# Overlapped dilated and neighbourhood attention: values copied in DRAM by blocks of 32 columns, dilated values in two loads, a later bias fill and two staging tiles

## Chip, cores and metric

The kernel runs on one core of one Trainium2 chip. The metric is the device time of one execution in microseconds (us), compared as the median of several runs. An execution is also profiled, and every row below is from that one.

## The reference

A whole two-block network on 1024 tokens of width 1024. The first block (retention, a state space branch, cross attention) is not touched. The second block projects the normalised tokens to queries, keys and values of two attentions with 8 heads each, normalises both outputs, multiplies them by `w_out`, and ends with a mixture of experts:

```python
p_dil = proj[..., :3 * WIDTH_DIL].reshape(B, S, 3, N_HEADS_DIL, HEAD_DIM).transpose(2, 0, 3, 1, 4)
p_na = proj[..., 3 * WIDTH_DIL:].reshape(B, S, 3, N_HEADS_NA, HEAD_DIM).transpose(2, 0, 3, 1, 4)
y_dil = dilated_mixture_attention(p_dil[0], p_dil[1], p_dil[2], slopes)
y_na = neighbourhood_attention(p_na[0], p_na[1], p_na[2], rpb[layer])
y_dil = rms_norm_2(y_dil.transpose(0, 2, 1, 3).reshape(B, S, WIDTH_DIL), g_out_dil[layer])
y_na = rms_norm_2(y_na.transpose(0, 2, 1, 3).reshape(B, S, WIDTH_NA), g_out_na[layer])
h = h + jnp.concatenate([y_dil, y_na], axis=-1) @ w_out[layer]
```

The dilated attention lets a token see keys at distances 1, 4 and 16 apart inside windows. The neighbourhood attention lays the tokens on a grid of 16 rows by 64 columns; a token sees 8 rows by 16 columns, with a learned bias for each offset.

## The kernel before

Everything in float32, by three matmuls per product (a high part and a low part of each operand: `mm3`, lines 181 to 183). Heads are worked in four pairs. A scheduler orders each engine's instructions by a simulated timeline, so that work of one function stands between that of others; each engine then takes its own list strictly in order.

Around the change, in order of time:

- `na_bias` (line 1281) builds the table of biases on GpSimd and writes it to DRAM: `e_scr` (the learned values) and `b_scr` (all biases and -1e30 where nothing is seen). `na_bias_row` copies 16 rows from `e_scr` to `b_scr`. All these transfers are issued by GpSimd, while `values` makes the dilated values tile by tile (`v_f`) and SyncE stores them to `vd_scr`.
- `dilated` (line 1091) loops over pairs. In a round it scores the present pair (`scores`, 16 pieces: 8 windows of 32 positions, then 8 of the 4 residues), and turns, splits and multiplies the pair before (`scale` on GpSimd, `flip`, `gather`). `load_values` (line 1145) fetches the values of a piece from `vd_scr` into a tile `dv`; 3 are fetched a round ahead, the others 3 steps ahead. `project` makes the next pair's queries and keys, and `filler` other work: in round 0 the neighbourhood's values, stored to `vn_scr`; in rounds 1 to 3 its queries and keys (`na_project`), each through the tile `n_`, of which there is one.
- After pair 3 is scored, the last dilated round runs beside `neighbour` (line 1317): 32 steps (2 blocks of rows, 4 pairs, 4 blocks of columns), each scores, softmax, turn (`flip` into `npT`, 3 tiles) and multiply (`gather`). For a step `load_values` (line 1346) fetches a tile `nv` from `vn_scr`, 8 ahead. Each pair's output goes through a tile `nyo` that takes a buffer of `npT`, and is stored to `yn_scr` by SyncE. `mix_out2` multiplies by `w_out` in between.

SyncE issues nearly all loads and stores, in one list. A load into a buffer in use holds up what is behind it. The two loads that the change is about read

```python
src = vt[:, lo:hi, z.pr].rearrange("(c r) x f -> r x c f", r=2)                                    # dv, L1152
src = v_scr[pr].rearrange("(r x) c i f -> r x c (i f)", x=64)[:, k0s[j % 4]:k0s[j % 4] + 32, rb:rb + 3]  # nv, L1350
```

so that the outermost dimension of the source has 2 steps for a `dv` of a window and 4 for an `nv`.

Of the kernel before, what the change touches and what calls it, by code (L numbers as in the profile page):

```python
# [10 lines left out]
F32 = mybir.dt.float32  # L11
# [108 lines left out]
class Net:  # L120
# [970 lines left out]
    def dilated(self, hn, v_scr, yd_scr, g, acc, filler):  # L1091

        nc = self.nc
        with ExitStack() as es:
# [144 lines left out]
            def tiles():  # L1239
                sq, o = (wk.tile([P, 2, 512], F32R, name=name, tag="dpT", bufs=3) for name in ("dsq", "dyo"))  # L1240
                return sq[:, 0].bitcast(F32), o

            def spare():
                sq = wk.tile([P, 2, 2, 256], F32, name="dsq", tag="db2", bufs=1).rearrange("p a b x -> p (a b x)")[:, :512]
                return sq, single("dyo")

            def single(name):
                return cp.tile([P, 2, 512], F32R, name=name, tag="n_")

            prev = None  # L1250
            for pr in range(PAIRS + 1):
# [30 lines left out]
                filler(pr, lambda: wk.tile([P, 2, 2, P], F32R, name="v_f", tag="dv", bufs=6), single)  # L1282
                prev = z


    def na_bias(self, e_scr, b_scr):


        nc = self.nc
        with self.pool("nb", 1, side="right") as wk:  # L1290
# [15 lines left out]
            nc.gpsimd.memset(neg, NEG)  # L1306
            for half, r0, r1, k0 in ((0, 0, 8, 8), (0, 5, 8, 0), (1, 0, 8, 0), (1, 0, 4, 8)):
                to = b_scr[:, half, 16 * r0:16 * r1, k0:k0 + 4].rearrange("q p r t k -> p q (r t k)")
                nc.gpsimd.dma_start(to, neg[16 * r0:16 * r1, None].to_broadcast(list(to.shape)))

    def na_bias_row(self, e_scr, b_scr, row):

        half, r = divmod(row, 8)
        rs = min(max(row - 4, 0), 8)
        self.nc.gpsimd.dma_start(b_scr[:, half, 16 * r:16 * r + 16, rs - 4 * half:rs - 4 * half + 8].rearrange("q c r t k -> q c (r t k)"),
                                 e_scr[:, :, rs - row + 7:rs - row + 15].rearrange("q c r h t k -> q c (r h t k)"))

    def neighbour(self, qn_scr, kn_scr, v_scr, yn_scr, b_scr, g, acc):

        nc = self.nc  # L1320
        with ExitStack() as es:
            cp = es.enter_context(self.pool("nc", 1, side="left"))
            qp = es.enter_context(self.pool("nq", 2, side="left"))
            k0s = (0, 8, 24, 32)
            sets = [(cp.tile([P, 2, 12, 64], F32R, name=f"nkbd{i}"), cp.tile([P, 12, 2, 3, 32], F32, name=f"nbias{i}")) for i in range(2)]
# [102 lines left out]
    def mix_out2(self, wk, res, x3_scr, y_scr, acc, ready):  # L1428
# [13 lines left out]
        for side in range(2):  # L1442
# [3 lines left out]
            for n in range(NT):  # L1446
                y = coming
                if n + 1 < NT:
                    coming = fetch(side * NT + n + 1)
                if n % 4 == 0:  # L1450
                    r = self.rsqrt_mean(acc[side][:, n:n + 4], 512)
                for cb in range(2):
                    cs = slice(cb * 512, cb * 512 + 512)
                    po = self.bank("m")
                    self.mm3(po, lambda k: (y[k][:, 0], y[k][:, 1]), lambda k: (ws[cb][0][:, k], ws[cb][1][:, k]), range(PAIRS))
                    nc.vector.scalar_tensor_tensor(res[n][:, cs], po, r[:, n % 4:n % 4 + 1], res[n][:, cs], op0=OP.mult, op1=OP.add)
                    yield
# [405 lines left out]
    def build(self, upto=99):  # L1863
# [7 lines left out]
        with ExitStack() as es:  # L1871
# [48 lines left out]
            yd_scr, yn_scr = (scr(n + "_scr", [P, PAIRS, 2, S]) for n in ("yd", "yn"))  # L1920
            vd_scr, vn_scr = scr("vd_scr", [S, PAIRS, 2, P]), scr("vn_scr", [PAIRS, 256, 4, 2, P])
            gd, gn = (self.gain(n) for n in ("g_out_dil_2", "g_out_na_2"))
            acc = [self.cp.tile([P, NT], F32, name=f"acc{i}") for i in range(2)]
            qn_scr, kn_scr = scr("qn_scr", [PAIRS, P, 2, 2, 512]), scr("kn_scr", [PAIRS, P, 2, S])
            right = ExitStack()
# [5 lines left out]
            right.close()  # L1931
            self.na_bias(e_scr, b_scr)

            def filler(k, values, halves):
                if k == 0:
                    def dst(n, cb):
                        return vn_scr[2 * cb:2 * cb + 2, n % 2 * P:n % 2 * P + P, n // 2].rearrange("h p i f -> p h (i f)")
                    for _ in self.values(hn, 2560, dst, values):
                        pass
                for row in ((), range(8), range(8, 16), (), ())[k]:  # L1940
# [31 lines left out]
```

## Time and profile before

| | |
|---|---|
| three runs | 2391.97, 2394.05, 2394.61 us; median 2394.05 |
| the profiled execution | 2393.05 us, of which the span from first to last instruction is 2391.3 |
| busy in the span | TensorE (PE) 88%, VectorE (DVE) 53%, ScalarE (ACT) 40%, GpSimd (POOL) 24% |
| mean granted clock of TensorE | 0.932 of full speed |
| moved by DMA | 341.36 MB, 143 GB/s over the span |

TensorE is the engine with the most work, so the stages to look at are those in which it stands idle. A profile gives for every idle time of an engine what ended it. [...]

### The profile page before, as it was taken

What the parts mean: (1) busy time and instruction counts of PE and PEld (TensorE: products, weight loads), DVE (VectorE), ACT (ScalarE), POOL (GpSimd) and SP (SyncE); (2) the same over time, 40 slices, a digit from 0 to 9 for tenths busy, and PEclk for the clock granted to TensorE, in tenths of its full rate; (3) what the DMA queues carried; (4) which work ended last, traced back from release to release, by engine and by line L of the source; (5) the groups of instructions that cost most, each with busy time, mean ns of one, the idle gap of its engine ahead of it and who ended that gap; (6) DMA issues with size and microseconds to landing.
All of it is one profiled execution on the core that took longest, in us unless ns stands there. A gap on an engine that the chain in (4) does not pass through costs nothing. (4 is left out here: it accounts for less than half of the span.)

```text
span 2391.3 us, 35907 instructions
## 1 busy us (share of the span) xinstructions
PE 2104.5 (88%) x13327; PEld 1881.4 (79%) x13327; DVE 1267.0 (53%) x2830; ACT 953.8 (40%) x1831; POOL 566.1 (24%) x683
## 2 busy tenths in 40 slices
PE   6999999999999999999987997999648679769991
PEld 6889999999979989989987796878537567657881
DVE  7418677866634353444353433455426345747785
ACT  6423444343452231343152434365324233246662
POOL 1134545543310020010033131313313222011105
PEclk9999999999999999999998998999768788779996
DMA  6542232223266333311228323323357651178996
GB/s 226 200 147 61 66 96 71 69 65 89 55 212 209 102 130 115 124 58 49 89 99 267 105 80 103 133 91 125 137 165 223 203 166 43 76 248 310 339 318 246
DMA packets 263620, 341.36 MB, mean 143 GB/s; under 512 B 48081, under 2 KB 211832, under 8 KB 262416
## 3 DMA queue, kind: packets, MB, share of 16 engines
q1 hardware_dynamic: 240352, 267.90, 35.0%
q0 software_dynamic: 16448, 50.67, 6.5%
q10 hardware_dynamic: 6640, 20.45, 2.2%
q8 instruction: 107, 1.75, 0.3%
q14 instruction: 73, 0.60, 0.1%
HBM read 247.68 MB, written 93.34 MB: 143 GB/s over the span
## 5 line engine op out<-in xcount | busy, mean ns | idle before, releaser
L155 DVE TENSOR_TENSOR wlo<-wraw,whi 128x1024 fp32r<-128x1024 f32 x222 | 274.2, 1240 | 283.7 <-ACT whi L154 281.9
L154 ACT CAST whi<-wraw 128x1024 fp32r<-128x1024 f32 x224 | 234.2, 1051 | 445.6 <-PE psm L183 168.3
L181 PE MATMUL psm<-whi,h_lo 128*128 128x256 f32 x768 | 223.5, 291 | 5.9 <-DVE ropeB L367 2.7
L182 PE MATMUL psm<-wlo,h_hi 128*128 128x256 f32 x768 | 220.2, 287 | 0.0
L183 PE MATMUL psm<-whi,h_hi 128*128 128x256 f32 x768 | 220.0, 286 | 0.0
L181 PEld LDWEIGHTS psm<-whi,h_lo 128*128 128x128 f32 x768 | 146.8, 191 | 8.9 <-issue 2.9
L182 PE MATMUL psm<-h_lo,whi 128*128 128x512 f32 x384 | 151.6, 395 | 0.0
L183 PE MATMUL psm<-h_hi,whi 128*128 128x512 f32 x384 | 150.9, 393 | 0.0
L181 PE MATMUL psm<-h_hi,wlo 128*128 128x512 f32 x384 | 149.6, 394 | 0.0
L182 PEld LDWEIGHTS psm<-wlo,h_hi 128*128 128x128 f32 x768 | 146.9, 191 | 1.3 <-issue 0.8
L183 PEld LDWEIGHTS psm<-whi,h_hi 128*128 128x128 f32 x768 | 146.8, 191 | 1.0 <-issue 0.8
L181 PE MATMUL psm<-hn_hi,wlo 128*128 128x512 f32 x256 | 104.3, 407 | 15.5 <-DVE n__16817 L1054 11.7
L182 PE MATMUL psm<-hn_lo,whi 128*128 128x512 f32 x256 | 103.3, 403 | 0.0
L183 PE MATMUL psm<-hn_hi,whi 128*128 128x512 f32 x256 | 102.8, 402 | 0.0
L181 PE MATMUL psm<-whi,hn_lo 128*128 128x256 f32 x256 | 76.7, 300 | 13.9 <-DVE v_f L155 11.3
L1722 POOL DMA_INDIRECT xg<-hf_scr,rt_table x23 | 24.0, 1044 | 254.4 <-PE pst L1732 178.5
L181 PEld LDWEIGHTS psm<-h_hi,wlo 128*128 128x128 f32 x384 | 72.2, 188 | 14.7 <-issue 0.2
L183 PEld LDWEIGHTS psm<-h_hi,whi 128*128 128x128 f32 x384 | 72.2, 188 | 14.4
L182 PEld LDWEIGHTS psm<-h_lo,whi 128*128 128x128 f32 x384 | 72.2, 188 | 13.8
L1373 POOL TENSOR_TENSOR np<-np,nrd 128x768 f32<-128x768 f32 x32 | 46.6, 1465 | 149.4 <-DVE nrd L1372 129.3
L181 PE MATMUL psm<-whi,xl 128*128 128x512 f32 x184 | 76.6, 417 | 3.7 <-DVE xl L155 3.7
L845 DVE TENSOR_TENSOR res<-psm,res 128x256 f32<-128x256 f32 x64 | 27.0, 424 | 99.5 <-PE psm L183 98.1
(645 smaller groups left out, 6555.5 us busy)
## 6 DMA issues: line engine op xcount, KB each, us to landing
wraw<-w_in SPq DMA_DIRECT2D x40, 512.0 KB
wraw<-w_gate SPq DMA_DIRECT2D x64, 256.0 KB
wraw<-w_up SPq DMA_DIRECT2D x64, 256.0 KB
wraw<-w_down SPq DMA_DIRECT2D x32, 512.0 KB
wraw<-w_in SPq DMA_DIRECT2D x48, 256.0 KB
wraw<-w_out SPq DMA_DIRECT2D x24, 512.0 KB
nv<-vn_scr SPq DMA_DIRECT2D x32, 384.0 KB
y_all<-ye ACTq DMA_DIRECT2D x23, 512.0 KB
```

What stands on the lines that cost most here:

```text
L154: nc.scalar.copy(hi, src)
L155: (eng or nc.vector).tensor_tensor(lo, src, hi.bitcast(F32), op=OP.subtract)
L181: self.nc.tensor.matmul(ps, ll, rh, start=start and j == 0, stop=False)
L182: self.nc.tensor.matmul(ps, lh, rl, start=False, stop=False)
L183: self.nc.tensor.matmul(ps, lh, rh, start=False, stop=stop and j == n - 1)
L845: self.nc.vector.tensor_tensor(res[n][:, cs], ps, res[n][:, cs], op=OP.add)
L1373: nc.gpsimd.tensor_tensor(p, p, rd[:, :, None].to_broadcast([P, 2, 384]), op=OP.mult)
L1722: nc.gpsimd.indirect_dma_start(g, None, hf_scr[:, :], bass.IndirectOffsetOnAxis(ap=table[:, slot:slot + 1], axis=0))
```

## The change

1. The neighbourhood's values are stored as `vn_scr` [256, pair, 4, 2, 128], and 16 transfers issued by GpSimd copy them from DRAM to DRAM into `vw_scr`: for each of the four blocks of columns a copy of its 32 columns in 4 rows. An `nv` is then 128 rows of one stride.
2. A dilated window's values come in two loads, one for each half of the partitions. There are 4 buffers `dv` instead of 6, one is fetched a round ahead instead of 3, and the others 1 step ahead instead of 3.
3. The tile `n_` is doubled. The squares `dsq` of a dilated output take the buffer of the bias `db2` instead of one of `dpT`.
4. The fill of `b_scr` with -1e30 is written from DRAM (`n_scr`) in round 1's filler, and the bias rows are copied with 16 steps outermost instead of 4.
5. `mix_out2` takes the reciprocal root of the dilated half once for all 8 tiles.

```diff
-                v = wk.tile([P, 2, 2, P], F32R, name="dv", tag="dv", bufs=6)
+                v = wk.tile([P, 2, 2, P], F32R, name="dv", tag="dv", bufs=4)
                 k = P
                 if j < 8:
                     lo, hi = max(32 * j - 16, 0), min(32 * j + 48, 256)
-                    k = 2 * (hi - lo)
-                    src = vt[:, lo:hi, z.pr].rearrange("(c r) x f -> r x c f", r=2)
+                    k = hi - lo
+                    src = [vt[r::2, lo:hi, z.pr].rearrange("c x f -> x c f") for r in range(2)]
                 else:
-                    src = vt[j - 8, :, z.pr].rearrange("(c x) f -> x c f", x=P)
-                nc.sync.dma_start(v[:k].rearrange("p c i f -> p c (i f)").bitcast(F32), src)
+                    src = [vt[j - 8, :, z.pr].rearrange("(c x) f -> x c f", x=P)]
+                for r, x in enumerate(src):
+                    nc.sync.dma_start(v[r * k:r * k + k].rearrange("p c i f -> p c (i f)").bitcast(F32), x)
...
+            def squared():
+                return wk.tile([P, 2, 2, 256], F32, name="dsq", tag="db2", bufs=1).rearrange("p a b x -> p (a b x)")[:, :512]
...
-                return cp.tile([P, 2, 512], F32R, name=name, tag="n_")
+                return cp.tile([P, 2, 512], F32R, name=name, tag="n_", bufs=2)
...
-                            if i == (j if j < 8 else 2 * j - 8) - 3:
+                            if i == (j if j < 8 else 2 * j - 8) - 1:
...
-                    for j in range(3):
-                        load_values(z, j)
+                    load_values(z, 0)
...
+    def na_bias_fill(self, n_scr, b_scr):
+
+        for half, r0, r1, k0 in ((0, 0, 8, 8), (0, 5, 8, 0), (1, 0, 8, 0), (1, 0, 4, 8)):
+            to = b_scr[:, half, 16 * r0:16 * r1, k0:k0 + 4].rearrange("q p r t k -> p q (r t k)")
+            self.nc.gpsimd.dma_start(to, n_scr[16 * r0:16 * r1, None].to_broadcast(list(to.shape)))
...
-        self.nc.gpsimd.dma_start(b_scr[:, half, 16 * r:16 * r + 16, rs - 4 * half:rs - 4 * half + 8].rearrange("q c r t k -> q c (r t k)"),
-                                 e_scr[:, :, rs - row + 7:rs - row + 15].rearrange("q c r h t k -> q c (r h t k)"))
+        self.nc.gpsimd.dma_start(b_scr[:, half, 16 * r:16 * r + 16, rs - 4 * half:rs - 4 * half + 8].rearrange("q c r t k -> c q (r t k)"),
+                                 e_scr[:, :, rs - row + 7:rs - row + 15].rearrange("q c r h t k -> c q (r h t k)"))
...
-                src = v_scr[pr].rearrange("(r x) c i f -> r x c (i f)", x=64)[:, k0s[j % 4]:k0s[j % 4] + 32, rb:rb + 3]
-                nc.sync.dma_start(v[j].rearrange("p c i f -> p (c i f)").bitcast(F32), src.rearrange("r x c f -> r x (c f)"))
+                nc.sync.dma_start(v[j].rearrange("p c i f -> p (c i f)").bitcast(F32), v_scr[j % 4, :, pr, rb:rb + 3].rearrange("p c i f -> p (c i f)"))
...
+                for cb in ((), (), range(4), (), ())[k]:
+                    for r in range(4):
+                        nc.gpsimd.dma_start(vw_scr[cb, 32 * r:32 * r + 32].rearrange("p q c i f -> p q (c i f)"),
+                                            vn_scr[64 * r + WINDOWS[cb]:64 * r + WINDOWS[cb] + 32].rearrange("p q c i f -> p q (c i f)"))
```

Three places show what the scheduler makes of it (a row is a line of the kernel, an operation, what it writes and reads, its size, and how often it stands there in succession; lines are those of each kernel's own file).

SyncE, where the last stores of the neighbourhood's values (`vn_scr`) meet the values of dilated pair 0 (`dv`) and the next weights (`wraw`), before:

```order
L1026 DMA vn_scr<-v_f 128x2x256
L1155 DMA dv<-vd_scr 128x2x256 x2
L1026 DMA vn_scr<-v_f 128x2x256
L1155 DMA dv<-vd_scr 128x2x256 x2
L1155 DMA dv<-vd_scr 96x2x256
L1155 DMA dv<-vd_scr 128x2x256
L170 DMA wraw<-w_in 128x4x128 x2
L1130 DMA db_15412<-k_dil_b 128x512
```

and of the changed kernel:

```order
L1027 DMA vn_scr<-v_f 128x2x256
L1157 DMA dv<-vd_scr 64x2x256 x2
L1027 DMA vn_scr<-v_f 128x2x256
L1157 DMA dv<-vd_scr 64x2x256 x4
L171 DMA wraw<-w_in 128x4x128 x2
L1157 DMA dv<-vd_scr 64x2x256 x6
L1157 DMA dv<-vd_scr 48x2x256 x2
L1131 DMA db_15428<-k_dil_b 128x512
```

The two weight loads stood behind six tiles of values and stand behind three; a tile of a window is two rows now.

SyncE, where the neighbourhood begins (`nv`, `nq`, `nkbd` and `nbias` are its values, queries, keys and biases), before:

```order
L1155 DMA dv<-vd_scr 128x2x256
L1155 DMA dv<-vd_scr 96x2x256
L1155 DMA dv<-vd_scr 128x2x256 x3
L170 DMA wraw<-w_out 128x2x512
L1351 DMA nv<-vn_scr 128x1x768 x8
L1333 DMA nq<-qn_scr 128x1024
L1334 DMA nkbd_16930<-kn_scr 128x2x768
```

and of the changed kernel:

```order
L1157 DMA dv<-vd_scr 64x2x256 x6
L1157 DMA dv<-vd_scr 48x2x256 x2
L171 DMA wraw<-w_out 128x2x512
L1356 DMA nv<-vw_scr 128x768 x8
L1339 DMA nq<-qn_scr 128x1024
L1340 DMA nkbd_16970<-kn_scr 128x2x768
```

The order is the same, with one tile of `dv` fewer ahead of the eight `nv`; what changed is the shape of the transfers.

GpSimd, the transfers of the bias and of the copy (`st1r` belongs to `merge`, which joins the two softmaxes of pair 1), before:

```order
L1309 DMA b_scr<-nb_neg 128x4x768
L1309 DMA b_scr<-nb_neg 48x4x768
L1309 DMA b_scr<-nb_neg 128x4x768
L1309 DMA b_scr<-nb_neg 64x4x768
L1303 DMA e_scr<-nb_e 15x16x96 x8
L1315 DMA b_scr<-e_scr 4x16x1536 x16
```

and of the changed kernel, in two pieces:

```order
L1309 DMA n_scr<-nb_neg 128x768
L1305 DMA e_scr<-nb_e 15x16x96 x8
L1315 DMA b_scr<-n_scr 128x4x768
L1315 DMA b_scr<-n_scr 48x4x768
L1315 DMA b_scr<-n_scr 128x4x768
L1315 DMA b_scr<-n_scr 64x4x768
L1321 DMA b_scr<-e_scr 16x4x1536 x16
...
L1183 COPY st1r<-st_14447 32x4x2 x8
L1953 DMA vw_scr<-vn_scr 16x8192 x16
L1183 COPY st1r<-st_14447 32x4x2 x8
```

The fill moved from ahead of `e_scr` to behind it, and the 16 copies stand in the middle of `merge` of pair 1.

## Rows read from the trace of the kernel before

**Rows 1.** Page, first line.
```profile
span 2391.3 us, 35907 instructions
```

**Rows 2.** Windows by stage: engines' busy us (instructions), granted clock, DMA share, GB/s.
```profile
1240.00:1340.00 100.00, 79.57 (x519) 73.27 (x520) 40.55 (x82) 37.21 (x65) 36.40 (x82) 0.86 0.72 233
1340.00:1400.00 60.00, 52.55 (x235) 43.51 (x234) 29.30 (x103) 31.77 (x86) 20.73 (x49) 0.89 0.20 62
...
1440.00:1480.00 40.00, 26.20 (x143) 22.38 (x142) 10.57 (x34) 12.30 (x38) 3.10 (x16) 0.86 0.32 101
1480.00:1680.00 200.00, 192.34 (x1004) 160.67 (x1003) 108.87 (x346) 105.74 (x274) 54.67 (x116) 0.98 0.34 113
1680.00:1720.00 40.00, 25.28 (x110) 21.53 (x109) 14.63 (x55) 10.30 (x18) 17.89 (x20) 0.66 0.25 93
1720.00:1985.00 265.00, 177.98 (x962) 146.93 (x961) 110.89 (x324) 95.12 (x247) 67.06 (x79) 0.80 0.60 191
...
2160.00:2320.00 160.00, 158.28 (x766) 128.13 (x765) 125.05 (x154) 106.40 (x155) 15.41 (x15) 1.00 0.98 334
```

**Rows 3.** TensorE's waits, 1720 to 1985: total us, times, longest.
```profile
PE pst L1381 <- DVE npT L155: 34.2, 5, 18.7
PE psa L181 <- DMA nkbd<-kn_scr: 26.5, 2, 23.4
PE pso L181 <- DMA nv<-vn_scr: 10.8, 2, 10.4
```

**Rows 4.** ScalarE's longest wait in the same stretch.
```profile
ACT npT L154 <- DMA yn_scr<-nyo: 53.1, 4, 25.0
```

**Rows 5.** SyncE's timeline where the neighbourhood begins: start, us, issues in succession.
```profile
1726.18 16.76 SPq L1155 DMA_DIRECT2D dv<-vd_scr  x5
...
1743.86 24.00 SPq L1351 DMA_DIRECT2D nv<-vn_scr  x8
```

**Rows 6.** Windows of 10 us, columns as in rows 2.
```profile
1266.00:1276.00 10.00, 6.21 (x46) 5.97 (x45) 0.00 (x0) 0.00 (x0) 0.60 (x1) 0.84 1.01 265
...
1455.00:1465.00 10.00, 8.71 (x43) 6.96 (x42) 0.48 (x1) 0.00 (x0) 0.00 (x0) 1.00 0.14 48
...
1750.00:1760.00 10.00, 4.54 (x23) 3.88 (x23) 3.97 (x9) 5.25 (x14) 1.47 (x1) 0.54 0.26 102
...
1490.00:1500.00 10.00, 9.85 (x56) 8.34 (x55) 7.70 (x23) 6.23 (x14) 2.00 (x7) 1.00 0.13 47
```

**Rows 7.** DMA issues: count, KB each, and us from issue to landing for GpSimd's.
```profile
nv<-vn_scr SPq DMA_DIRECT2D x32, 384.0 KB
...
b_scr<-e_scr POOLq DMA_DIRECT2D x16, 384.0 KB, 10.6
```

**Rows 8.** TensorE's timeline, its longest gaps from 1270 to 1710, in brackets.
```profile
1280.94 0.58 PE L181 MATMUL psm<-whi,hn_lo 128*128 128x256 f32 x1 [8.73 <-DVE v_f L155]
...
1477.51 0.58 PE L181 MATMUL pso<-dpT,dv 128*128 128x256 f32 x1 [13.80 <-ACT dy L1233]
...
1707.94 0.77 PE L181 MATMUL psm<-hn_hi,wlo 128*128 128x512 f32 x1 [11.70 <-DVE n__16817 L1054]
```

**Rows 9.** SyncE's timeline where pair 0's values are loaded.
```profile
1451.72 15.78 SPq L1155 DMA_DIRECT2D dv<-vd_scr  x4
1467.55 2.59 SPq L170 DMA_DIRECT2D wraw<-w_in  x2
```

**Rows 10.** ScalarE's timeline at the same gaps.
```profile
1280.06 0.37 ACT L154 CAST v_f<-psm 128x256 fp32r<-128x256 f32 x1 [15.18 <-DMA vd_scr<-v_f]
...
1475.98 1.04 ACT L154 CAST whi<-wraw 128x1024 fp32r<-128x1024 f32 x1 [21.23 <-DMA wraw<-w_in]
...
1706.02 0.60 ACT L1051 ACTIVATE n__16817<-psm 128x512 fp32r<-128x512 f32 x1 [8.26 <-DMA yd_scr<-dyo]
```

**Rows 11.** GpSimd's timeline: the bias transfers, and `merge` of pair 1.
```profile
1253.47 2.79 POOL L1309 DMA_DIRECT2D b_scr<-nb_neg  x4
...
1482.86 0.88 POOL L1180 COPY st2n<-st 32x8 f32<-32x8 f32 x4 [30.40 <-ACT dp L1170]
```

More of the change, by code (lines that the diff above doesn't have):

```diff
@@ L35 @@
 HK = 1
+WINDOWS = (0, 8, 24, 32)
 def shape_constants():
@@ L1239, in tiles @@
             def tiles():
-                sq, o = (wk.tile([P, 2, 512], F32R, name=name, tag="dpT", bufs=3) for name in ("dsq", "dyo"))
-                return sq[:, 0].bitcast(F32), o
+                return squared(), wk.tile([P, 2, 512], F32R, name="dyo", tag="dpT", bufs=3)
+            def squared():
+                return wk.tile([P, 2, 2, 256], F32, name="dsq", tag="db2", bufs=1).rearrange("p a b x -> p (a b x)")[:, :512]
             def spare():
-                sq = wk.tile([P, 2, 2, 256], F32, name="dsq", tag="db2", bufs=1).rearrange("p a b x -> p (a b x)")[:, :512]
-                return sq, single("dyo")
+                return squared(), single("dyo")
             def single(name):
-                return cp.tile([P, 2, 512], F32R, name=name, tag="n_")
+                return cp.tile([P, 2, 512], F32R, name=name, tag="n_", bufs=2)
             prev = None
@@ L1277, in dilated, with na_bias @@
                 if z:
-                    for j in range(3):
-                        load_values(z, j)
+                    load_values(z, 0)
                 if pr + 1 < PAIRS:
                     project(pr + 1)
-                filler(pr, lambda: wk.tile([P, 2, 2, P], F32R, name="v_f", tag="dv", bufs=6), single)
+                filler(pr, lambda: wk.tile([P, 2, 2, P], F32R, name="v_f", tag="dv", bufs=4), single)
                 prev = z
-    def na_bias(self, e_scr, b_scr):
+    def na_bias(self, e_scr, n_scr):
         nc = self.nc
@@ L1306, in na_bias @@
             nc.gpsimd.memset(neg, NEG)
-            for half, r0, r1, k0 in ((0, 0, 8, 8), (0, 5, 8, 0), (1, 0, 8, 0), (1, 0, 4, 8)):
-                to = b_scr[:, half, 16 * r0:16 * r1, k0:k0 + 4].rearrange("q p r t k -> p q (r t k)")
-                nc.gpsimd.dma_start(to, neg[16 * r0:16 * r1, None].to_broadcast(list(to.shape)))
+            nc.gpsimd.dma_start(n_scr, neg)
+    def na_bias_fill(self, n_scr, b_scr):
+        for half, r0, r1, k0 in ((0, 0, 8, 8), (0, 5, 8, 0), (1, 0, 8, 0), (1, 0, 4, 8)):
+            to = b_scr[:, half, 16 * r0:16 * r1, k0:k0 + 4].rearrange("q p r t k -> p q (r t k)")
+            self.nc.gpsimd.dma_start(to, n_scr[16 * r0:16 * r1, None].to_broadcast(list(to.shape)))
     def na_bias_row(self, e_scr, b_scr, row):
@@ L1323, in neighbour @@
             qp = es.enter_context(self.pool("nq", 2, side="left"))
-            k0s = (0, 8, 24, 32)
+            k0s = WINDOWS
             sets = [(cp.tile([P, 2, 12, 64], F32R, name=f"nkbd{i}"), cp.tile([P, 12, 2, 3, 32], F32, name=f"nbias{i}")) for i in range(2)]
@@ L1449, in mix_out2 @@
                     coming = fetch(side * NT + n + 1)
-                if n % 4 == 0:
-                    r = self.rsqrt_mean(acc[side][:, n:n + 4], 512)
+                if n == 0 or n == 4 and side:
+                    r = self.rsqrt_mean(acc[side][:, n:n + 4] if side else acc[0], 512)
                 for cb in range(2):
@@ L1455, in mix_out2 @@
                     self.mm3(po, lambda k: (y[k][:, 0], y[k][:, 1]), lambda k: (ws[cb][0][:, k], ws[cb][1][:, k]), range(PAIRS))
-                    nc.vector.scalar_tensor_tensor(res[n][:, cs], po, r[:, n % 4:n % 4 + 1], res[n][:, cs], op0=OP.mult, op1=OP.add)
+                    nc.vector.scalar_tensor_tensor(res[n][:, cs], po, r[:, n % r.shape[1]:n % r.shape[1] + 1], res[n][:, cs], op0=OP.mult, op1=OP.add)
                     yield
@@ L1876, in build @@
             e_scr, b_scr = scr("e_scr", [PAIRS, 16, 15, 2, 3, 32]), scr("b_scr", [PAIRS, 2, P, 12, 6, 32])
+            n_scr = scr("n_scr", [P, 768])
             kv_scr = scr("ka_scr", [P, KD, 256]), scr("va_scr", [P, 2, D])
@@ L1931, in build @@
             right.close()
-            self.na_bias(e_scr, b_scr)
+            self.na_bias(e_scr, n_scr)
             def filler(k, values, halves):
@@ L1936, in dst @@
                     def dst(n, cb):
-                        return vn_scr[2 * cb:2 * cb + 2, n % 2 * P:n % 2 * P + P, n // 2].rearrange("h p i f -> p h (i f)")
+                        return vn_scr[n % 2 * P:n % 2 * P + P, 2 * cb:2 * cb + 2, n // 2].rearrange("p h i f -> p h (i f)")
                     for _ in self.values(hn, 2560, dst, values):
                         pass
-                for row in ((), range(8), range(8, 16), (), ())[k]:
+                if k == 1:
+                    self.na_bias_fill(n_scr, b_scr)
+                for row in ((), range(16), (), (), ())[k]:
                     self.na_bias_row(e_scr, b_scr, row)
+                for cb in ((), (), range(4), (), ())[k]:
+                    for r in range(4):
+                        nc.gpsimd.dma_start(vw_scr[cb, 32 * r:32 * r + 32].rearrange("p q c i f -> p q (c i f)"),
+                                            vn_scr[64 * r + WINDOWS[cb]:64 * r + WINDOWS[cb] + 32].rearrange("p q c i f -> p q (c i f)"))
                 for pr in ((),(0,1),(2,),(3,),())[k]:
@@ L1947, in build @@
             hp_es.close()
-            na = self.neighbour(qn_scr, kn_scr, vn_scr, yn_scr, b_scr, gn, acc[1])
+            na = self.neighbour(qn_scr, kn_scr, vw_scr, yn_scr, b_scr, gn, acc[1])
             next(na)
```

3 lines of the change are left out of this document (2 added, 1 removed).

## The prediction

> **What bounds the kernel now.** I read the windows by stage first, since an average over 2391 us [rows 1] says nothing of one stage. Between the untouched first block and the untouched experts lie five stages that the change reaches, and TensorE's idle time in each is the width less its busy time [rows 2]: 1240 to 1340 (bias traffic beside the dilated values) 100 - 79.6 = 20.4 us; 1340 to 1400 60 - 52.6 = 7.4; 1440 to 1480 13.8; 1680 to 1720 14.7; and 1720 to 1985, where both attentions run, 265 - 178 = 87. From 1480 to 1680 TensorE idles 7.7 us in 200: there it is the bound and nothing can be won. So some 143 us of idle time are at stake, three fifths of them in one stage.
>
> Next I read what ends the waits of that stage. TensorE waits 34.2 us for `npT`, 26.5 for the keys `nkbd` and 10.8 for `nv` [rows 3], 71.5 of the 87. The first of these is a transfer too: ScalarE cannot refill `npT` until the store of `nyo`, which sits in an `npT` buffer, has landed, 53.1 us in four times [rows 4]. So all three are late transfers. They are late though the DMA engines are on average only 0.60 busy at 191 GB/s; the experts run at 0.98 and 334 [rows 2]. Why shows in short windows: from 1750 to 1760, in the middle of the eight `nv` issues that took SyncE 24.00 us [rows 5], the share is 0.26 at 102 GB/s, a quarter of the engines; when window values `dv` are all that moves, 0.14 and 0.13 at 48 and 47 GB/s, an eighth [rows 6]. These are the 4 and the 2 steps of the outermost dimension in their sources: four of 16 engines carry an `nv`, two a `dv`; and since eight `nv` in a row bring no more than a quarter, it is the same four each time.
>
> [...]
>
> **The big stage, 1720 to 1985.** What those four engines carry: 32 `nv` of 384 KB [rows 7], a quarter each is 98 KB, at 102/4 = 25.5 GB/s 3.9 us, together 123 us. The stage moves 191 x 265 = 50.6 MB; the other 38.0 MB, spread over 16 engines at 334/16 = 20.9 GB/s, take each engine 114 us. So four engines have work for 237 of 265 us, and everything that is spread over 16 must wait for its part on these four: the keys, the store of `nyo`. That is the bound. After the change an `nv` is 128 rows and goes to 16 engines, and the stage needs 50.6/334 = 152 us of each. TensorE's 178 busy us become the bound. I leave 25 us idle: the 87 - 71.5 = 15.5 that no late transfer made, and 10 for bursts, since transfers would still fill three quarters of the stage. Gain 62. Bounds: 25, if only the first `nv` and half of the wait for keys go (10.4 + 13); 80, if all three waits go and part of the clock comes back (0.80 granted here, 0.98 in 1480 to 1680 [rows 2]).
>
> **Two staging tiles.** At 1707.94 TensorE waits 11.7 us for a bank that is read out into `n_` [rows 8]. ScalarE in turn waits there 8.26 us for the store of `dyo`, which uses the one `n_` buffer, for its second half after the first [rows 10]. With two buffers the halves do not wait for each other, and the first buffer is free again about when the second half was written before, one store (8 us) and one wait earlier: gain 10, bounds 5 (half) and 11.7. The new user of `db2` makes that bias load wait for the squares; it is needed only by the ninth piece of the next round, which covers it.
>
> **Values of pairs 0 to 2.** From 1340 to 1400, three `dv` loaded ahead share engines with weight loads; one is left, on 16 engines. TensorE idles 7.4 us there; I take 5, bounds 0 and 7.4. With 4 buffers instead of 6 a `dv` can be fetched only four pieces ahead; a round of 16 pieces lasts about 100 us (two rounds in 1480 to 1680), so 6 us a piece cover a load of a few us, and I cost it at nothing.
>
> **The bias fill.** GpSimd issues the fill at 1253 [rows 11] and from 1266 to 1276 all DMA engines are full, while ScalarE and VectorE do nothing [rows 6]: a store of `v_f`, issued by SyncE behind earlier work, takes so long that ScalarE waits 15.18 us for its buffer [rows 10] and TensorE 8.73 [rows 8]. Now the fill stands behind `e_scr` and a round trip of `n_scr`. The order shows that "later" is some 5 us, not a round: GpSimd has nothing else to do. The weight loads and the first stores then get ahead of it. But its 4.5 MB (368 x 4 x 768 numbers by the order) and the rows' 6.3 MB (16 x 384 KB [rows 7]) follow each other without the gap that `e_scr` made before. Gain 7, bounds -5 and 10.
>
> **The copy.** 16 transfers of 16 x 8192 numbers by the order are 8.4 MB, read and written once more, on GpSimd's queue, in the middle of `merge` of pair 1. They wait for the last `vn_scr` store, which SyncE issues ahead of the `dv` of 1451.72 [rows 9]: about 1451. At 334 GB/s it takes 25 us, at the 265 of the crowded window [rows 6] 32: until 1476 to 1483. GpSimd itself is covered, since its next step waits until 1482.86 in any case [rows 11]. SyncE is not. Just then it issues the values of pair 0 and weights. Before, four `dv` on two engines each take it 15.78 us, the weights behind them are issued at 1467.55 [rows 9], ScalarE stands at their cast 21.23 us [rows 10], and TensorE idles 13.8 [rows 8]. These `dv` would now be out in a few us, which would return all of the 13.8; but they meet the copy, and what a store met at 1266 (15 us instead of a few) they meet too. If SyncE's transfers end only with the copy, weights land at 1477 to 1484 and the stall is 14 to 21 us. I take 19, so a loss of 5; bounds: a gain of 13 (copy does not hurt) and a loss of 15.
>
> [...]
>
> **The sum.** 62 + 10 + 5 + 7 - 5 = 79 us off the profiled execution's 2393.05 (span 2391.3 and 1.75 around it) is 2314; the median lies 1.0 above that execution, so I say 2315. The single root in `mix_out2` saves a chain of VectorE operations of a few hundred ns and is left out. The order inside other stages changes little.
>
> **Rivals.**
>
> *The next limit comes soon.* In the big stage the chain scores, softmax, GpSimd's scaling, turn, multiply has few buffers (three `npT`, one shared with `nyo`), SyncE's list stays in order, and 152 us of transfers come in bursts. For it: `nbias` and `nkbd` of two pairs come together. Against: TensorE runs at 96% in 1480 to 1680 with the same chain in the dilated part. Gain there 25 instead of 62: 2352. Chance 18%.
>
> *The copy holds SyncE's queue.* The whole 32 us pass before pair 0's values and weights land, and TensorE, out of work at about 1455, waits to 1487: 32 less the 13.8 of before, 18 lost instead of 5. 2328. It does not change the sign and lies in my range; I count it with the forecast.
>
> *More comes back.* Copy hidden, 80 in the big stage, 7.4 and 11.7 and 10 in the others, 13 at pair 0: 122 us, 2272. For it: the clock was at 0.66 to 0.80 only where TensorE idled. Chance 12%.
>
> *The transfers do not spread.* If the number of engines does not follow the outermost dimension, only `n_` and the fill are left and the copy costs: 10 + 7 - 5 = 12, so 2382; with the copy at its worst no change. Chance 6%; the three shares speak against it.
>
> *Slower: the copy itself runs on few engines.* Its rows are contiguous over the whole block, so how it is cut decides. On four engines (102 GB/s) it lasts 82 us, on two (48) 175. Everything that SyncE sends over 16 engines waits for these. The stall grows by copy length less the 27 us from 1451 to 1478; the other parts gain 84, so it turns at a copy of 111 us, 76 GB/s. On two engines: 84 - 148 = 64 us slower, 2458. Against it: the order shows the copy as 16 rows. Chance 4%.
>
> **How the numbers follow.** The forecast with the copy rival has 60%, at 2315, own range 2295 to 2335. Smaller and larger gain add 18 and 12, no spread 6, slower 4. To leave out two in ten I reach on the low side to 2283, half of "more comes back", and on the high side to 2356, all of "the next limit". A measurement of this kernel tells 0.2%, 5 us, from no change. Faster by more than that: 60 + 18 + 12 and most of no spread, 0.94; slower 0.04; the same 0.02.
>
> **What would show it.** In the changed profile: a share near 1 or bursts in place of 0.26 while `nv` load, eight issues in some 5 us instead of 24; the waits for `npT`, `nkbd` and `nv` mostly gone; the stage from 1720 about 200 us long with TensorE at 85 to 90%; no wait before `n_` of more than 3 us; the store of `v_f` no longer waited for 15 us; around 1455 to 1480 a stall as long as before or longer, with GpSimd's transfers filling the engines. I would be wrong if the big stage stays over 240 us, or if the stall beside the copy exceeds 35.

## The result, and the profile after

The changed kernel takes 2310.26 us (median of four runs, 2300.61 to 2312.33), against 2393.61 for the kernel before beside it: a ratio of 0.9644, 95% interval 0.9617 to 0.9672. The forecast was 2315. The profiled execution took 2309.05 us; its page begins:

```profile
span 2307.3 us, 35968 instructions
```

The span is 84.0 us shorter [rows 1]. Windows over the stages that answer to [rows 2] (columns as there):

```profile
1247.00:1347.00 100.00, 82.09 (x528) 75.22 (x529) 40.65 (x83) 37.86 (x66) 35.50 (x84) 0.88 0.72 241
1347.00:1397.00 50.00, 46.35 (x223) 38.93 (x222) 28.97 (x103) 30.81 (x85) 20.20 (x49) 0.97 0.17 53
1445.00:1495.00 50.00, 27.78 (x113) 22.00 (x112) 9.39 (x27) 12.80 (x37) 10.27 (x28) 0.68 0.76 241
1495.00:1690.00 195.00, 189.11 (x1001) 159.11 (x1000) 109.02 (x348) 106.24 (x269) 56.61 (x116) 0.98 0.35 114
...
1722.00:1930.00 208.00, 196.75 (x1135) 161.49 (x1135) 129.66 (x349) 105.79 (x271) 78.18 (x88) 0.95 0.69 243
```

In the last row TensorE idles 11 us of 208, and its granted clock is 0.95 where it was 0.80. The third row is the one that got worse: 22 us idle in 50, DMA share (the mean of the 16 engines) 0.76. The waits of TensorE from 1720 to 1930 (total us, times, longest) that answer to [rows 3]:

```profile
PE psa L182 <- DMA nkbd<-kn_scr: 2.9, 1, 2.9
...
PE pst L1386 <- DVE npT L156: 1.7, 2, 1.3
...
PE pso L182 <- DMA nv<-vw_scr: 0.8, 1, 0.8
```

The 71.5 us are 5.4. SyncE's timeline has the eight `nv` in 4.43 us [rows 5], and, at the other place, the values of pair 0 [rows 9]:

```profile
1447.43 1.44 SPq L171 DMA_DIRECT2D wraw<-w_in  x2
1448.97 29.64 SPq L1157 DMA_DIRECT2D dv<-vd_scr  x8
...
1734.23 4.43 SPq L1356 DMA_DIRECT2D nv<-vw_scr  x8
```

Windows of 10 us, one as `nv` load, two beside the copy [rows 6]:

```profile
1745.00:1755.00 10.00, 8.92 (x63) 7.00 (x61) 5.99 (x18) 6.46 (x18) 2.78 (x2) 1.00 1.04 390
...
1460.00:1470.00 10.00, 4.72 (x16) 3.39 (x16) 1.25 (x5) 1.11 (x3) 2.21 (x7) 0.67 1.00 321
1470.00:1480.00 10.00, 0.93 (x4) 0.96 (x5) 0.80 (x1) 1.88 (x5) 0.00 (x0) 0.50 0.90 254
```

While `nv` load, the share is 1.04 (0.26 before); while the copy runs, it is 1.00 and 0.90, but TensorE is busy 4.72 and 0.93 of 10 us. Its gaps [rows 8] are now:

```profile
1283.81 0.58 PE L182 MATMUL psm<-whi,hn_lo 128*128 128x256 f32 x1 [6.28 <-DVE v_f L156]
...
1461.64 0.55 PE L182 MATMUL pso<-dpT,dv 128*128 128x256 f32 x1 [4.51 <-DMA dv<-vd_scr]
...
1479.07 0.55 PE L182 MATMUL pso<-dpT,dv 128*128 128x256 f32 x1 [11.86 <-DMA dv<-vd_scr]
```

The gap before `n_` is gone. Transfers in the 30 us of the copy, 1446 to 1476: queues (packets, MB, share of 16 engines), then issues (KB each, median us to landing):

```profile
q0 software_dynamic: 512, 8.39, 81.7%
q1 hardware_dynamic: 1710, 1.17, 14.8%
...
vw_scr<-vn_scr POOLq DMA_DIRECT2D x16, 512.0 KB, 12.5
dv<-vd_scr SPq DMA_DIRECT2D x9, 128.0 KB, 12.1
wraw<-w_in SPq DMA_DIRECT2D x2, 256.0 KB, 29.5
```

GpSimd's queue moves the whole copy, in packets of 16 KB (8.39 MB in 512), and SyncE's queue moves 1.17 MB.

To compare kernels I cut each trace at marks that all have: the first `vd_scr` store, the first and last `vn_scr` store, the first and last `qn_scr` store, the first `nkbd` matmul, the last `nsum` matmul, the `rt_ov` matmul, the end. Us between marks:

| | before | changed | difference |
|---|---|---|---|
| start to first `vd_scr` | 1264.3 | 1271.0 | +6.7 |
| A: to first `vn_scr` | 132.6 | 123.1 | -9.5 |
| to last `vn_scr` | 50.5 | 50.4 | -0.1 |
| B: to first `qn_scr` | 69.1 | 87.3 | +18.2 |
| C: to last `qn_scr` | 200.6 | 179.6 | -21.0 |
| to first `nkbd` | 12.0 | 10.8 | -1.2 |
| D: to last `nsum` | 295.5 | 207.6 | -87.9 |
| to `rt_ov` | 62.7 | 65.4 | +2.7 |
| X: to the end | 304.0 | 312.1 | +8.1 |

TensorE over D, before and changed, and over B, before and changed (columns as in [rows 2]):

```profile
1729.10:2024.60 295.50, 209.57 (x1127) 173.00 (x1127) 127.01 (x360) 104.89 (x269) 76.18 (x88) 0.81 0.53 167
1722.20:1929.80 207.60, 196.51 (x1133) 161.22 (x1134) 129.66 (x349) 105.59 (x271) 78.18 (x88) 0.95 0.69 243
...
1447.40:1516.50 69.10, 54.84 (x278) 46.15 (x277) 32.05 (x101) 29.22 (x77) 13.04 (x37) 0.90 0.28 88
1444.50:1531.80 87.30, 63.31 (x291) 51.52 (x290) 33.42 (x99) 32.14 (x79) 24.20 (x52) 0.78 0.51 159
```

In D the idle time falls from 85.9 to 11.1 us and the busy time by 13.1, at a granted clock of 0.95 instead of 0.81. In B the idle time grows from 14.3 to 24.0 us and the busy time by 8.5, at 0.78 instead of 0.90.

### The profile page after: what moved, and what is told of

It reads as the page before. It is cut to its first block, busy times and chain, and to the rows that moved or that the text cites. A ratio compares the mean times of both kernels' runs of the same rounds, so it can differ in the third digit from the quotient of the medians.

```text
span 2307.3 us, 35968 instructions
## 1 busy us (share of the span) xinstructions
PE 2103.0 (91%) x13327; PEld 1881.5 (82%) x13327; DVE 1268.7 (55%) x2819; ACT 956.9 (41%) x1831; POOL 576.2 (25%) x700
## 5 line engine op out<-in xcount | busy, mean ns | idle before, releaser
L182 PE MATMUL psm<-whi,hn_lo 128*128 128x256 f32 x256 | 76.9, 300 | 13.3 <-DVE v_f L156 10.8
L846 DVE TENSOR_TENSOR res<-psm,res 128x256 f32<-128x256 f32 x64 | 27.0, 424 | 103.1 <-PE psm L184 102.0
L182 PE MATMUL psm<-whi,s_lo 128*128 128x256 f32 x256 | 73.8, 288 | 4.7 <-DVE res L846 4.0
```

The costliest lines, as they stand in the source:

```text
L182: self.nc.tensor.matmul(ps, ll, rh, start=start and j == 0, stop=False)
L846: self.nc.vector.tensor_tensor(res[n][:, cs], ps, res[n][:, cs], op=OP.add)
```

## Experiments

Each was timed beside the kernel before, whose medians were 2394.97 to 2397.45. The same cuts for all of them (us):

| kernel | A | B | C | D | X | median |
|---|---|---|---|---|---|---|
| before | 132.6 | 69.1 | 200.6 | 295.5 | 304.0 | 2393.61 |
| before, `nv` in four loads (e1) | 131.2 | 68.9 | 200.6 | 227.4 | 305.1 | 2327.89 |
| before, `dv` in two loads (e12) | 127.7 | 51.9 | 185.8 | 287.3 | 304.7 | 2347.83 |
| changed | 123.1 | 87.3 | 179.6 | 207.6 | 312.1 | 2310.26 |
| no copy, `nv` in four loads (e2) | 124.1 | 53.7 | 180.7 | 228.8 | 312.9 | 2295.37 |
| copy moved, not held (e3) | 124.5 | 88.4 | 179.8 | 210.1 | 312.5 | 2311.24 |
| `dv` three ahead, one `n_` (e4) | 127.1 | 74.3 | 181.8 | 204.2 | 313.8 | 2293.51 |
| copy held until late (e5) | 124.1 | 53.6 | 181.0 | 214.5 | 310.7 | 2281.94 |
| `dv` in one load (e6) | 126.4 | 103.1 | 203.2 | 228.4 | 311.5 | 2365.59 |
| old fill (e7) | 124.6 | 85.7 | 182.3 | 210.5 | 301.3 | 2302.15 |
| copy in 2 KB rows (e8) | 124.0 | 67.1 | 180.1 | 209.1 | 307.4 | 2288.03 |
| late copy, old fill (e9) | 127.2 | 53.5 | 181.6 | 212.8 | 311.8 | 2280.04 |
| rows with `q` outermost (e10) | 123.6 | 87.1 | 179.1 | 211.2 | 310.0 | 2306.67 |
| one `n_` buffer (e11) | 124.2 | 87.0 | 184.7 | 208.5 | 312.3 | 2316.45 |

A row's stages are cut from one execution. Kernels whose edits do not touch a stage still differ there: by up to 2.6 us in A, 2.7 in B, 3.2 in C and 3.6 in D, so smaller differences prove nothing.

**e1: only the spread of `nv`.**

```diff
-nc.sync.dma_start(v[j]..., src.rearrange("r x c f -> r x (c f)"))
+for r in range(4):
+    nc.sync.dma_start(v[j][32 * r:32 * r + 32]..., src[r].rearrange("x c f -> x (c f)"))
```

> The kernel before, with one edit: each nv is read by four loads of 32 rows instead of one whose outermost dimension is 4. No copy, the same layout of vn_scr, the same bytes and the same 3 KB rows; dv stays on two engines. Theory (four engines carried every nv, and that set the big stage): TensorE's waits for npT, nkbd and nv go, the stage from the first nkbd matmul to the last nsum matmul falls from 295 us to about 215, and the kernel takes 2394 - 80 = 2314 us; if the dv of pair 3, still on two engines, hold up some of it, 2330. Rival (the copy's layout, or the eight separate issues, made the gain): the stage stays near 290 and the time near 2390, or is worse, since SyncE issues 96 loads more at about half a microsecond.

Ratio 0.970 (0.9679 to 0.972). D falls by 68.1 us, the rest stays. TensorE's waits in D:

```profile
PE pso L181 <- DMA nv<-vn_scr: 10.4, 1, 10.4
PE psa L181 <- DMA nkbd<-kn_scr: 9.9, 2, 8.1
...
PE pst L1382 <- DVE npT L155: 1.8, 2, 1.3
```

The waits for `npT` and `nkbd`, of other transfers, fall from 34.2 and 26.5 us to 1.8 and 9.9, by an edit of `nv` alone. The wait for the first `nv` stays; in SyncE's list these stand behind five `dv`, which take 17.82 us there. The rival (the copy's layout made the gain) falls for these 68 us. Of the two numbers expected it is the second, 2330: D stays 19.8 us longer than in the changed kernel, and e2 and e6 show what these need.

One thing e1 leaves open. The store of `nyo`, for which `npT` waited, took SyncE 5.15 us to issue before (median of four) and 0.38 in e1. So part of the waiting was in SyncE's list, and e1 does not part it from the waiting on the four engines.

**e2: no copy; e3: the copy moved; e4: `dv` loaded further ahead.** Three kernels that tell the copy from the shallow loading of `dv` as the cause of the stall in B. e2 drops the copy and takes `nv` from `vn_scr` as e1 does; e3 and e4:

```diff
+def copy_step(k, i):                      # e3; called behind scores(z, i - 2)
+    if k == 3 and i < 16: nc.gpsimd.dma_start(vw_scr[...], vn_scr[...])
-    if i == (j if j < 8 else 2 * j - 8) - 1:                       # e4
+    if i == (j if j < 8 else 2 * j - 8) - 3:
-    load_values(z, 0)
+    for j in range(3): load_values(z, j)   # and dv bufs=6, n_ bufs=1
```

> The changed kernel without the copy: each nv is read from vn_scr by four loads of 32 rows, everything else as changed. Theory (the copy's traffic is what made the stage around it 18 us longer): the gaps of 4.5 and 11.9 us before the first qn_scr store go, the first qn_scr store lies some 18 us earlier counted from the last vn_scr store, and the time is 2310 - 18 = 2292 us. Rival (the values of pair 0, only one of them loaded ahead and four buffers, make the stall): the two gaps stay and the time is 2308 to 2312. Second rival (three quarters more issues on SyncE hold up the big stage): stall gone, but the big stage 10 or more longer, 2300 to 2310.

> The changed kernel with the copy moved: its 16 transfers are issued one by one in the scoring round of pair 3 (about 1580 to 1690), one behind each piece's scores, instead of all in a row at 1446. Theory (a burst of 8.4 MB meets SyncE's queue; the same bytes spread over a round do not): the stall before the first qn_scr store goes, no new one above 4 us comes in the round of pair 3, and the time is 2310 - 16 = 2294 us. Rival (the copy costs its bytes wherever it stands): the stall is found in the later round instead, 2305 to 2310. Rival of the values loaded too late: the first stall stays, 2308 to 2312.

> The changed kernel with the copy left as it is, but dv loaded ahead as before the change: six buffers and three loads ahead of a round; n_ has one buffer again, since both do not fit. Theory (the copy makes the stall): the first qn_scr store stays about as late after the last vn_scr store as in the changed kernel, 87 us; the single n_ buffer costs about 10 us at the third pair of queries and keys; 2318 to 2322 us. Rival (loading too late makes it): the distance falls to the 69 us of before or less, and the time is 2300 to 2306 in spite of n_.

e3 tested nothing: the copy waits for nothing but the `vn_scr` stores, and GpSimd's order again has it ahead of the round. Its tile `vw_scr` in e3's trace (count, shortest/median/longest ns, first to last issue):

```profile
L1958 POOL DMA_DIRECT2D vw_scr<-vn_scr x16: 486/486/547, 1449.1 to 1467.0; - x16
```

Without the copy B is 53.7, so the copy costs 33.6 us there, nearly twice the 18 that I had expected of it. With the copy but `dv` three ahead, B is 74.3: 13.0 of the 33.6 come back. So neither rival was right alone: the copy makes loads late, and one load ahead leaves nothing in hand. Without a copy the depth does not matter (53.7 in e2 with four buffers, 51.9 in e12 with six).

e2 as a whole is only 15 us faster, since D is 21 us longer than with the copied layout, as the second rival had it. Windows of its first 150 us in D, and SyncE's issues there:

```profile
1690.00:1840.00 150.00, 124.59 (x706) 103.98 (x707) 86.02 (x249) 70.75 (x189) 55.00 (x67) 0.85 0.91 286
```

```profile
1702.80 17.00 SPq L1358 DMA_DIRECT2D nv<-vn_scr  x32
```

and the same 150 us of the changed kernel:

```profile
1722.00:1872.00 150.00, 141.52 (x817) 116.77 (x818) 97.18 (x276) 79.08 (x207) 60.79 (x73) 0.93 0.86 308
```

Four loads of 96 KB instead of one of 384 take SyncE 17.00 us instead of 4.43 for eight tiles, and in these 150 us fewer bytes move (286 GB/s against 308) with busier engines (0.91 against 0.86). In D TensorE waits for `npT` and `dv`, where the changed kernel has 1.7 us for the one and nothing above 0.3 for the other:

```profile
PE pst L1389 <- DVE npT L156: 9.9, 4, 7.7
PE psm L182 <- DMA dv<-vd_scr: 6.8, 2, 5.8
```

So, with `dv` spread, the copy does buy something, 21 us in D.

**e5: the copy held until late; e8: its packets made smaller.**

```diff
+def copy_step(k, i, m):                   # e5; m: one score of the piece just made
+    if k in (2, 3) and i % 2 == 0:
+        cb, r = divmod(8 * (k - 2) + i // 2, 4)
+        nc.gpsimd.dma_start(vw_scr[cb, 32 * r:32 * r + 1, 0, 0, 0, 0:1], m)
+        nc.gpsimd.dma_start(vw_scr[cb, 32 * r:32 * r + 32]..., vn_scr[...])
+for c in (0, 2):                          # e8
+    nc.gpsimd.dma_start(vw_scr[cb, 32 * r:32 * r + 32, :, c:c + 2]..., vn_scr[..., :, c:c + 2]...)
```

> The changed kernel with the copy held back: eight of its 16 transfers stand in the scoring round of pair 2 and eight in that of pair 3, one behind every second piece's scores; each is held by a 4-byte write of one of those scores into its target, which the copy then overwrites. Theory (the burst of copies beside the values of pair 0 makes the stall; DMA engines are half idle in the two later rounds): the first qn_scr store follows the last vn_scr store by about 54 us, as without the copy, no new TensorE gap over 4 us between 1500 and 1720, the big stage stays at 207, and the time is 2310 - 33 = 2277 us, 2270 to 2287. Rival (a copied byte costs the same wherever it is copied): the 33 us come back as late values of pairs 1 and 2 or late weights, 2300 to 2310. A second: GpSimd, which issues them and also scales, is held up by the waits, 2290 to 2300.

> The changed kernel with the copy at the same place and of the same bytes, but in 32 transfers of 128 rows of 2 KB instead of 16 of 16 rows of 32 KB, which the trace shows as packets of 16 KB. Theory (an engine's time goes by packets in turn between queues, so big packets of the copy push SyncE's 1 KB packets back): the values of pair 0 get a larger part of the engines, the distance from the last vn_scr store to the first qn_scr store falls from 87 to 65 to 75 us, 2290 to 2300. Rival (bytes count, whatever the packets): 85 to 90 us and 2308 to 2314, or later if smaller packets copy more slowly.

e5 holds: B is 53.6 and C 181.0, against 53.7 and 180.7 without a copy (e2), and the kernel takes 2281.94 (ratio 0.9527, 0.9497 to 0.9556). The copied bytes, issued from 1532.5 to 1661.5, cost nothing in these rounds, where the DMA share is 0.35 in the changed kernel (fourth row of the windows above). D is 214.5, and 212.8 in e9, which copies as late, against 207.6 to 211.2 in the kernels that copy early with four `dv` buffers: what these 2 to 7 us are I did not find.

e8 leaves the copy's bytes as they are, but not its place. It splits the copy along the third dimension of `vn_scr`, so that half of the transfers wait for the earlier `vn_scr` stores only, and 16 of the 32 are issued before the last store (at 1447.2). GpSimd's first issues of either half:

```profile
1417.42 4.20 POOL L1954 DMA_DIRECT2D vw_scr<-vn_scr  x8 [13.28 <-DMA vn_scr<-v_f]
...
1449.59 4.13 POOL L1954 DMA_DIRECT2D vw_scr<-vn_scr  x8 [4.55 <-DMA vn_scr<-v_f]
```

B falls to 67.1 and the kernel takes 2288.03. Transfers of the 30 us from 1448 to 1478, with the second half of the copy:

```profile
q0 software_dynamic: 1280, 4.20, 45.6%
q1 hardware_dynamic: 4410, 3.14, 36.7%
```

SyncE's queue gets 3.14 MB instead of 1.17 through in the same time, and the copy's packets are 3.3 KB instead of 16; but the copy has half the bytes there too. The two causes part in 5 us in which both kernels have the copy running and weights of SyncE's on the way, 1460 to 1465, the changed kernel first:

```profile
q0 software_dynamic: 96, 1.57, 102.7%
q1 hardware_dynamic: 96, 0.05, 3.3%
...
q0 software_dynamic: 401, 1.31, 76.1%
q1 hardware_dynamic: 709, 0.41, 30.0%
```

Beside a copy that moves 1.31 MB instead of 1.57, SyncE's queue gets 0.41 through instead of 0.05. So the bytes of the other queue alone do not account for what SyncE's loads got here; its packets were 3.3 KB instead of 16. How much of the 20.2 us that B fell is due to it, and how much to the half that was copied earlier, e8 does not tell. TensorE no longer waits for `dv` there; its longest wait, 13.9 us, is for `dy`, which ScalarE copies behind the cast of weights for which it waited 18.05 us.

e8's theory has an engine's time go by packets in turn between queues. In the changed kernel the two queues' packets agree with it, 96 and 96 in these 5 us, 94 and 92 in the 5 us before, 95 and 95 in the 5 us behind. In e8 they are 401 and 709, so equal turns are not shown there.

**e6 and e12: the spread of `dv`.** e6 puts the single load with two outermost steps back into the changed kernel; e12 puts two loads into the kernel before (the lines are e12's; e6 goes the other way):

```diff
-src = vt[:, lo:hi, z.pr].rearrange("(c r) x f -> r x c f", r=2)
+src = [vt[r::2, lo:hi, z.pr].rearrange("c x f -> x c f") for r in range(2)]
```

> The changed kernel with each window's dv again in one load whose outermost dimension is 2; four buffers, one load ahead and the copy as changed. Theory (two engines carry it, and it meets the copy with only one load ahead): the stall before the first qn_scr store grows by 10 to 30 us and the big stage by up to 10, as pair 3's window values queue before it; 2325 to 2350 us. Rival (only the nv mattered, dv hides behind TensorE's work): 2308 to 2314 us.

> The kernel before with one edit: each window's dv in two loads of 32 to 64 rows; six buffers, three loaded ahead, nv as before, no copy. By the prediction dv in two loads is worth 5 us in the values of pairs 0 to 2 and up to 13.8 at pair 0: 2376 to 2390. Theory by the run with dv in one load (which cost 55 us): the stretch from the first to the last qn_scr store falls from 200.6 to about 185, the one before it from 69 to about 54, and with some of the big stage 2394 - 31 = 2363, down to 2345 us.

e6 is 55 us slower than the changed kernel, more than I expected; e12 is 48 faster than the one before beside it (ratio 0.9799, 0.9775 to 0.9823), near the theory's lower end and far from the prediction's 5. In e6 SyncE (timeline) takes 22.92 us for three `dv` beside and behind the second half of the copy, and in D TensorE waits for the first `nv` as in e1:

```profile
1474.04 22.92 SPq L1153 DMA_DIRECT2D dv<-vd_scr  x3
...
PE pso L182 <- DMA nv<-vw_scr: 10.4, 1, 10.4
```

So the last 20 us of D need two edits together. With `nv` off the four engines D is 227.4 (e1), 228.8 when `dv` is spread too but `nv` comes in four loads (e2), 228.4 when `nv` is copied but `dv` is not spread (e6), and 207.6 only with `dv` spread and `nv` copied.

e12 shortens A by 4.9, B by 17.2, C by 14.8 and D by 8.2. In C half of it is the wait before `n_`; waits of TensorE from 1500 to 1687, and from 1697 to 1986:

```profile
PE psm L181 <- DVE n__16844 L1054: 4.5, 1, 4.5
...
PE pst L1382 <- DVE npT L155: 35.5, 5, 21.1
PE psa L181 <- DMA nkbd<-kn_scr: 26.8, 2, 24.4
```

The gap of 11.7 [rows 8] is 4.5 with one `n_` still: the store of `dyo` for which ScalarE waited [rows 10] was itself late beside `dv` on two engines. ScalarE issues it at 1699.77 on a queue of its own (q10) and goes on at 1706.02; in e12 these are 2.8 us apart instead of 6.3. Queues in the kernel before from 1699.7 to 1702, then from 1702 to 1705.4:

```profile
q10 hardware_dynamic: 222, 0.45, 50.8%
...
q10 hardware_dynamic: 47, 0.07, 5.6%
q1 hardware_dynamic: 101, 0.10, 8.6%
```

Most of the store, 0.45 MB, moves in 2.3 us. The last 0.07 MB take 3.4 us more, while all that moves beside them is `dv`, and both queues together have 14.2% of the engines, where `dv` alone has 0.13 to 0.14 [rows 6]. I read this as the 0.07 MB sharing the two engines of `dv`, though on another queue than SyncE's; no row shows single engines. In D the waits for `npT` and `nkbd` stay: `nv` is the first bound there.

**e7, e9, e10, e11: the small parts.** Old fill; old fill with e5's late copy; the rows with `q` outermost; one `n_`.

```diff
-nc.gpsimd.dma_start(n_scr, neg)                               # e7, e9
+nc.gpsimd.dma_start(to, neg[16 * r0:16 * r1, None].to_broadcast(list(to.shape)))
-rearrange("q c r t k -> c q (r t k)")                          # e10
+rearrange("q c r t k -> q c (r t k)")
-cp.tile([P, 2, 512], F32R, name=name, tag="n_", bufs=2)        # e11
+cp.tile([P, 2, 512], F32R, name=name, tag="n_", bufs=1)
```

> The changed kernel with the bias fill put back: four transfers straight from the tile nb_neg ahead of the rows, without n_scr. Theory: the wait of TensorE for v_f near 1284 grows from 6 to about 9 us and the distance from the first vd_scr store to the first vn_scr store from 123 to 126 to 130; 2313 to 2317 us. Rival (the fill's place hides anyway): same distance, 2308 to 2312.

> The late copy (held back by scores of pairs 2 and 3) together with the old bias fill straight from nb_neg. If both add up: 2282 - 8 = 2274 us. Theory: the old fill saved nothing where it stands (124.6 against 123.1 us from the first vd_scr store to the first vn_scr store); what it saved lay in the experts, whose instruction order happened to come out otherwise (301 us from the rt_ov matmuls to the end, 312 with the new fill), and such luck need not come again: 2278 to 2284, with 310 us there. Rival: 2270 to 2276, with 301 to 304 us there.

> The changed kernel with the sixteen bias rows again written with the pair q as outermost dimension (4 steps) instead of the column c (16 steps); fill, n_scr and the rest as changed. Theory (what the stretch from the first vd_scr store to the first vn_scr store gained, 132.6 to 123.1 us, came from the rows being spread over more engines, since the fill has been shown to give nothing and dv in two loads 2 to 3): the stretch is 129 to 132, and the time 2316 to 2320 us. Rival (fewer dv loaded ahead gave it): 123 to 125 us and 2308 to 2314.

> The changed kernel with one n_ buffer. By the prediction's term the second buffer is worth 10 us: a gap of some 10 us before the third pair's second half, the stretch from the first to the last qn_scr store 190 instead of 180, 2320 us. Rival, by the run with six dv buffers and one n_ (181.8 us for that stretch, a gap of 5): 2 to 5 us, 2312 to 2316.

e7: A is 124.6 against 123.1, and 127.2 in e9 against 124.1 in e5, so the new fill is worth 1.5 to 3.1 us, hardly more than the spread of 2.6. TensorE's longest wait for `v_f` does grow as expected, from 6.3 to 10.2, but all its waits for `v_f` in A only from 10.8 to 12.4. That the kernel is 8 us faster comes mostly from X, 301.3 against 312.1, which the fill does not touch; e9, with the same fill, has 311.8 there, and 2280.04 (ratio 0.9515, 0.9489 to 0.9541), the same as e5. e10: A is 123.6, nothing, and 2306.67; my theory on the rows fell. e11: C is 5.1 longer. ScalarE's timeline there has the wait of [rows 10] at half its length:

```profile
1705.65 0.60 ACT L1052 ACTIVATE n__16857<-psm 128x512 fp32r<-128x512 f32 x1 [4.10 <-DMA yd_scr<-dyo]
```

## Why the prediction came out right

The time and the main mechanism were right; of the terms, two were too small and three too favourable, and stages without a term cost 17.5 us. That the sum came within 5 us (79 against 84) is luck: these errors offset each other.

- **The big stage: mechanism right, 62 where 88 was measured, above the upper bound of 80.** e1 shows 68.1 from `nv` alone, close to the term. The step that was mis-sized is what TensorE would still spend there: "I leave 25 us idle", with its 178 busy us kept. Over D, which runs 40 us further than the stage and has 2.8 of them idle, 85.9 us idle became 11.1, a gain of 74.8 instead of 62. Another 13.1 came from the same matmuls at a granted clock of 0.95 instead of 0.81, which I had put into the upper bound alone. The account of the four engines also left out that the window values of pair 3 (five in 16.76 us [rows 5]) load two engines; put back into the changed kernel they cost 20.8 us in D (e6). The doubled tile, the buffer of `dsq` and the single root show no gain of their own here (67.1 off D in e6, which has all of them, 68.1 in e1, which has none); the last two were not run alone. That an `nv` of 128 rows would go to all 16 engines was my estimate from the shares of 0.26 with 4 outermost steps and 0.13 to 0.14 with 2 [rows 6]; measured is a share of 1.04 with 128.
- **Dilated values: 5, and 13.8 counted with the copy, where 4.9 + 17.2 + 14.8 + 8.2 = 45.1 were there** (e12, all stages; half of the 14.8 is the wait before `n_`). The failed step reads "from 1480 to 1680 TensorE idles 7.7 us in 200: there it is the bound and nothing can be won", with dilated values costed only where TensorE idled beside them, from 1340 to 1400. That spread transfers wait for the few busy engines, which I used for `nv`, I did not apply to `dv`: the store of `dyo` in C is late beside `dv` too (6.3 us, 2.8 in e12).
- **Four `dv` buffers at nothing:** right without the copy, wrong beside it, 13.0 us (e4). The cover named, a round's 6 us a piece, was there; but loads took 12.1 us beside the copy, and 3.1 in the same 30 us without it (e2).
- **The copy.** The length was right (estimate 25 to 32 us; issued from 1446, engines 0.90 to 1.00 busy until 1480), the price was not: I took a stall of 19 against 13.8, net 5. Net it was 18.2, just what the rival "the copy holds SyncE's queue" said, and in part by luck: the rival had 18 us more idle, and 9.7 of the 18.2 are idle time, 8.5 busy time at a lower clock (0.78 against 0.90). Run by run it is 17.2 won (e12) and 33.6 lost (e2). That rival's mechanism, SyncE's loads pushed back by the copy's, is shown by e2 and e5, in which the stall is gone, and by the time to landing of `dv` (12.1 us beside the copy, 3.1 in e2); the part of the packets by the 5 us beside e8. The copy did spread over the engines (1.00 at 321 GB/s), so the slower rival had no ground.
- **Two staging tiles:** 10, measured 5.1 (e11); most of the rest of that wait belonged to `dv`.
- **The bias fill:** 7, measured 1.5 to 3.1 (e7, e9). A gained 9.5 all the same: 4.9 by `dv` in two loads (e12). That fewer of them ahead gave more is not shown (127.1 in e4 with three ahead, but 127.2 in e9 with one). The wait for `v_f` remains, 6.28 us in TensorE and 11.26 in ScalarE, where I had said that it would go.
- **Not foreseen:** +6.7 before the first `vd_scr` store, most of which is no effect of the change. e1 and e12, whose edits lie behind it, have TensorE's instruction order of before up to there and reach it at 1268.6 and 1270.7: the profiled execution of before was early by some 4 to 6 us. And +8.1 in X, which stays open: all three kernels built on before have 304.0 to 305.1, those on the changed one 301.3 to 313.8. The order of instructions there differs from kernel to kernel, though no edit touches it; but e8 and the changed kernel have the same TensorE order there and 307.4 and 312.1, so the order does not explain it all.

The forecast's sum in the terms as measured: A 9.5, C 21.0 and D 87.9 won, 1.2 and 0.1 beside them, less B 18.2, start 6.7, `rt_ov` 2.7 and X 8.1: 84.0.

## What to carry to other kernels

Loads at a DMA share of 0.26 and 0.14, four and two of 16 engines, cost more here than their own delay. With `nv` spread, TensorE's waits for `npT` and `nkbd` fell from 34.2 and 26.5 us to 1.8 and 9.9 (e1); with `dv` spread, ScalarE went on 2.8 us after it issued the store of `dyo` instead of 6.3, and C, where the tensor engine seemed to be the bound, fell by 14.8 (e12). So look for late stores and weights behind such loads. Loads fetched only one ahead were safe here without the copy (B 53.7 in e2, 51.9 with three ahead in e12); beside its burst B was 87.3, 74.3 with three ahead (e4), and 67.1 with copy packets of 3.3 KB instead of 16 and half of the copy earlier (e8). Move such a copy to a round whose DMA share is low (0.35 here), and hold it there by a dependence, since its place in the code did not hold it (e3): here that gave 2282 us (e5), 28 less than the change.

## What the runs showed of the hardware that was not expected

A DRAM copy in transfers of 16 rows of 32 KB went in packets of 16 KB and, in its 30 us, took 81.7% of the DMA engines' time while SyncE's queue, with packets of 0.7 KB (1.17 MB in 1710), got 14.8%. In 5 us of it 96 packets of each queue went through, 1.57 MB against 0.05; with copy packets of 3.3 KB (e8) it was 1.31 MB against 0.41. And in the first 150 us of D, with `nv` in loads of 96 KB (e2) the engines were busier than with loads of 384 KB (0.91 against 0.86) at a lower rate (286 against 308 GB/s).
